# Seven half products that go on accumulating in PSUM, with ScalarE as the copier and another order of products

## The chip, the core and the metric

The kernel runs on one core of a Trainium2 chip. The metric is the device time of one execution in microseconds (us). TensorE (PE in the profile, its weight loads PEld) multiplies and writes to the PSUM banks; VectorE (DVE), ScalarE (ACT) and GpSimd (POOL) work beside it, each through its own queue in order; SyncE (SP) issues most DMAs.

## What is computed

One step of a two-layer trunk over 1024 prompt tokens and 64 sample tokens: a Mamba-2 layer, then a layer of causal window sums, each with a gated mixer and a residual add, then a final norm. The part that matters here is the large projections:

```python
def ssd_branch(h, ...):
    zxbcdt = h @ w_in              # 1024 -> 6176: z (gate), x, B, C, dt
    ...
    xbc_act = jax.nn.silu(conv)    # a causal convolution of width 4 over x, B, C
    ...
def pool_branch(h, ...):
    uz = h @ w_in                  # 1024 -> 4096: u (2048 columns) and z (2048 columns)
    ...                            # window sums of u over 4, 8, 16 or 2 tokens; silu(z)
```

All of it is float32, and the outputs are float32 too.

## The kernel before

Activations lie with features on the 128 partitions and the 1088 tokens (TOK) along the free axis. A float32 product is made of three matmuls: weights and activations are each split into a rounded high part and the rest, and high x high, high x low and low x high are summed in PSUM.

**Pairs of output tiles by seven half products.** For 12 pairs of the front (the list FRONT: pairs "z" of the gate, pairs "b" and "x" that feed the convolution) and for 14 pairs of the pool layer (p = 2 to 15) two output tiles u and z of 128 x 1088 are made together in Winograd's form of Strassen's product: the inner size 1024 and the tokens are halved, and seven products of 128 x 512 by 512 x 544 take the place of eight. Their activation operands are called B11, B21, T2, T3, T1, T4 and B22; the T are sums of blocks that were made ahead. A half product is 24 matmuls of 128 x 272 (2 halves of the tokens, c = 0 and 1; 4 blocks of the inner size; 3 of the split): lines L980 to L982 in `product`. A pair is 168 matmuls.

**The weights.** `w_sums` is a generator: each `next` gives one half weight operand, in the order of the products. GpSimd forms the sums of weight blocks (L945, L946, L950, L952), and `split_half` makes the high part by a ScalarE copy (L174) and the low part by a subtraction on VectorE, or on GpSimd for two of every seven (L176). `product` asks for the operand three products ahead; there are four buffers for split operands (tags wh and wl, two each), so a split can be made when the product four before it is done.

**Evacuation.** `fast_pair` runs the products as B11, B21, T2, T3, T1, T4, B22, each into PSUM banks of its own (tags mm, tr, y, S: eight banks in all). ScalarE copies B11 to a tile `s` (L1006); after that VectorE adds each product's banks to `s`, to z or to u (the adds all stand at L991, in a helper), 14 adds of 128 x 272 a pair, one more where the sample tokens lie apart.

**Work behind a pair.** `after(x)` is called behind each product. In the front, behind B22 of a "b" or "x" pair, the convolution of both tiles is written (`proj_end`, `conv_tile`): per tile a ScalarE start (L351, a part of 1024 tokens and one of 64), three VectorE steps on each part (L349), and an activation on ScalarE (L352). Six of the 12 front pairs have it. Gate pairs take an activation (`z_chunk`, L862) and a store. In the pool layer `u_pool` follows a pair: a chain of window sums on VectorE (L845, L850, L852, L854) and a store. In the first two front pairs the steps of `dt_phase` are interleaved; the last ends in small transposes on TensorE.

**Order.** The program is traced into a scheduler, which fixes each engine's queue ahead of the run; the listing's order is its order of preference among what is ready. `issue_after` pins a few instructions. On the chip every queue then runs in order and waits on semaphores.

Of the kernel before, what the change touches and what calls it, by code (L numbers as in the profile page):

```python
# [7 lines left out]
F32 = mybir.dt.float32  # L8
F32R = mybir.dt.float32r
AF = mybir.ActivationFunctionType  # L10
# [4 lines left out]
P = 128  # L15
# [82 lines left out]
class Build:  # L98
# [837 lines left out]
    def w_sums(self, n):  # L936


        nc = self.nc
        for _ in range(n):  # L940
            u, z = self.stream_next_raw(), self.stream_next_raw()
            self.stream_raw(self.wpos)
            s = self.tp.tile([P, 8, P], F32, tag="sw", bufs=2, name=self.name("sw"))
            f, l = slice(0, 4), slice(4, 8)
# [8 lines left out]
            yield self.split_half(s[:, f])  # L953
            yield self.split_half(z[:, l])
            self.stream_raw(self.wpos + 1)
            yield self.split_half(s[:, l])

    def fast_init(self, n):
# [4 lines left out]
        self.X = {"B11": [(h[:, :HALF], l[:, :HALF]) for h, l in self.hn[:4]], "T1": [(h[:, HALF:], l[:, HALF:]) for h, l in self.hn[:4]],  # L963
                  "B21": [(h[:, :HALF], l[:, :HALF]) for h, l in self.hn[4:]], "B22": [(h[:, HALF:], l[:, HALF:]) for h, l in self.hn[4:]]}

    def product(self, tags, x):
        nc = self.nc
        if x not in self.X:
            self.X[x] = [(t[:, :HALF], t[:, HALF:]) for t in (self.T[int(x[1]), k] for k in range(4))]
        nxt = next(self.wgen, None)  # L970
        if nxt:
            self.wahead.append(nxt)
        else:
            self.stream_split(self.wpos)
        hi, lo = self.wahead.pop(0)
        ps = [self.pp.tile([P, 512], F32, tag=t, bufs={"mm": 3, "tr": 2, "y": 2, "S": 1}[t], name=self.name("st")) for t in tags]
        for c in range(2):
            t = slice(QUART * c, QUART * c + QUART)
            for k, (xh, xl) in enumerate(self.X[x]):
                nc.tensor.matmul(ps[c][:, :QUART], hi[:, k], xh[:, t], start=(k == 0), stop=False)  # L980
                nc.tensor.matmul(ps[c][:, :QUART], hi[:, k], xl[:, t], start=False, stop=False)  # L981
                nc.tensor.matmul(ps[c][:, :QUART], lo[:, k], xh[:, t], start=False, stop=(k == 3))  # L982
        return [q[:, :QUART] for q in ps]

    def fast_pair(self, u, z, after):


        nc, product = self.nc, self.product

        def add(out, x, y):  # L990
            nc.vector.tensor_tensor(out=out, in0=x, in1=y, op=ALU.add)  # L991

        def put(dst, half, c, x, y):
            t, o, rv = dst
            o += HALF * half + QUART * c
            n = QUART - NS if rv is not None and half and c else QUART
            add(t[:, o:o + n], x[:, :n], y[:, :n])
            if n < QUART:
                add(rv, *(v[:, n:].rearrange("p (b i) -> p b i", i=8) for v in (x, y)))

        cs = [slice(QUART * c, QUART * c + QUART) for c in range(2)]
        s = self.tp.tile([P, HALF], F32, tag="mt2", bufs=self.nmt2, name=self.name("u2"))
        z1 = z[0][:, z[1]:z[1] + HALF]
        ps = product(("mm", "mm"), "B11")
        for c in range(2):
            nc.scalar.activation(s[:, cs[c]], ps[c], AF.Copy)  # L1006
        after("B11")
        ps = product(("tr", "tr"), "B21")
        for c in range(2):
            put(u, 0, c, ps[c], s[:, cs[c]])  # L1010
        after("B21")
        ps = product(("y", "y"), "T2")
        for c in range(2):
            add(s[:, cs[c]], ps[c], s[:, cs[c]])
        after("T2")
        ps = product(("mm", "S"), "T3")
        for c in range(2):
            add(z1[:, cs[c]], ps[c], s[:, cs[c]])
        after("T3")
        ps = product(("mm", "mm"), "T1")  # L1020
        for c in range(2):
            add(s[:, cs[c]], ps[c], s[:, cs[c]])
            put(z, 1, c, ps[c], z1[:, cs[c]])
            after(f"z1{c}")
        after("T1")
        ps = product(("tr", "tr"), "T4")
        for c in range(2):
            put(z, 0, c, ps[c], z1[:, cs[c]])
            after(f"z0{c}")
        after("T4")  # L1030
        ps = product(("y", "y"), "B22")
        for c in range(2):
            put(u, 1, c, ps[c], s[:, cs[c]])
        after("B22")

    def fast_pairs(self, late):

        sl = self.slots
        self.fast_init(16 - PLAIN)
        for p in range(PLAIN, 16):  # L1040
            U, dst = self.u_begin(p), sl.get("pz")

            def after(x):
                if x in ("z01", "z11"):
                    a = HALF * int(x[1])
                    self.z_chunk(dst, dst[:, a:a + HALF], a, HALF)
                elif x == "T4":
                    self.z_store(p, dst)
                elif p == 15 and x in ("T2", "T3"):
                    sl.free(*[self.T[int(x[1]), k] for k in range(4)])  # L1050
                    if x == "T2":
                        self.group_load(0)
                elif p == 15 and x == "T1":
                    self.free_acts(self.hn[:4])

            self.fast_pair((U[0], 15, U[1][:, :, 15:23]), (dst, 0, None), after)
            if p - PLAIN < len(late):
                self.u_pool(p - PLAIN, late[p - PLAIN])
            if p < 15:
                self.u_pool(p, U)  # L1060
        self.free_acts(self.hn[4:])
        sl.free(*[self.T[4, k] for k in range(4)])
        return U

    def group_load(self, gi):

# [342 lines left out]
    def front_pairs(self, ops, dt):  # L1409

        nc, sl = self.nc, self.slots
        self.fast_init(len(FRONT))
        self.G, G = {}, None
        for n, (kind, g) in enumerate(FRONT):
            if kind == "z":
                ts = [sl.get("z") for _ in range(2)]
                outs = [(t, 0, None) for t in ts]
            else:
                if kind == "b":
                    self.G[g] = G = self.proj_open(g)  # L1420
                ii = 2 * (kind == "x")
                ts = [self.proj_begin(G, ii + i) for i in range(2)]
                outs = [(t, 3, t[:, 1027:1115].rearrange("p (b w) -> p b w", w=11)[:, :, 3:11]) for t in ts]

            def after(x):
                if kind == "z" and x in ("z01", "z11"):
                    a = HALF * int(x[1])
                    self.z_chunk(ts[1], ts[1][:, a:a + HALF], a, HALF)
                elif kind == "z" and x in ("B21", "B22"):
                    a = HALF * (x == "B22")  # L1430
                    self.z_chunk(ts[0], ts[0][:, a:a + HALF], a, HALF)
                    if x == "B22":
                        self.gate_store(2 * g, ts[0])
# [9 lines left out]
                if n == 0 and x in ("B11", "B21"):  # L1443
# [11 lines left out]
            self.fast_pair(*outs, after)  # L1455
        sl.free(*[self.T[4, k] for k in range(4)])

    def ssd_layer(self):
# [348 lines left out]
```

## Time and profile before

| | |
|---|---|
| median of 3 runs | 1625.97 us (1620.98 to 1626.91) |
| the profiled execution | 1625.1 us, span 1623.2 us |
| granted TensorE clock, mean | 0.995 |
| PE busy | 1594.8 us, 98% of the span, 12061 matmuls |
| PEld busy | 1519.9 us, 94% |
| DVE busy | 1290.4 us, 79% |
| ACT busy | 815.2 us, 50% |
| POOL busy | 497.8 us, 31% |

The front's 12 pairs stand between 95.75 and 354.5 us of the span, the pool layer's 14 pairs between 1051.58 and 1346.5 us. A row of the timeline gives start, duration, engine, line, operation, output and inputs by the program's names, shape and count; in square brackets stands the engine's idle time before it and who ended it. Consecutive rows of one line are merged, with the last end. A row of groups gives the busy sum and the mean of one instruction, then the idle time before them. Matmuls are pipelined, so the duration of one (288 ns) is longer than the distance to the next.

### The profile page before, as it was taken

The numbers are of one execution on the slowest core, as the hardware profiler recorded it, in microseconds if no ns is written. First come the engines' busy times: TensorE is split into PE (matmuls) and PEld (weight loads), VectorE is DVE, ScalarE is ACT, GpSimd is POOL, SyncE is SP. The second block draws the span as 40 slices with busy tenths as digits, with TensorE's granted clock in tenths as the row PEclk, the third lists the DMA queues.
The fourth block names the chain that finished last, engine by engine and source line by source line (L and its number), as shares of the span: only waits on it lengthen the run. The fifth ranks groups of instructions, "written<-read, shape, count | busy, mean of one in ns | idle before, by whom it ended". The sixth has DMA issues, their size and how long they took to land.

```text
span 1623.2 us, 30975 instructions
## 1 busy us (share of the span) xinstructions
PE 1594.8 (98%) x12061; PEld 1519.9 (94%) x12061; DVE 1290.4 (79%) x2140; ACT 815.2 (50%) x1565; POOL 497.8 (31%) x527
## 2 busy tenths in 40 slices
PE   8999999999999999999999999999999999999997
PEld 6899999998889898898899899999999999999997
DVE  6875779777787888889878867988899867577886
ACT  6653444357667667675555536632322233333364
POOL 0233556421221302120112222366667640000241
PEclk9999999999999999999999999999999999999999
DMA  9422232354554554678899633043333369665773
GB/s 348 163 99 82 94 110 71 107 198 128 194 161 159 166 190 134 215 226 295 272 333 313 216 130 112 29 143 111 103 108 100 134 206 362 181 159 182 160 175 121
DMA packets 122306, 275.60 MB, mean 170 GB/s; under 512 B 18192, under 2 KB 59312, under 8 KB 122160
## 3 DMA queue, kind: packets, MB, share of 16 engines
q1 hardware_dynamic: 118128, 260.91, 47.4%
q0 software_dynamic: 4032, 12.72, 4.5%
q8 instruction: 95, 1.56, 0.4%
q14 instruction: 51, 0.42, 0.1%
HBM read 201.12 MB, written 70.23 MB: 167 GB/s over the span
## 4 chain that ended last, share of the span: by engine, by line
PE 83%; DVE 6%; DMA 4%; issue 3%; ACT 3%; POOL 1%; SPq 0%; DVEq 0%; POOLq 0%; ACTq 0%
PE st L982 11%; PE st L980 11%; PE st L981 11%; PE mm L182 10%; PE mm L183 10%; PE mm L184 10%; PE op L1197 2%; PE op L1198 2%; PE op L1196 2%; PE y L609 2%; PE S L588 2%; PE y L613 1%; DMA acb<-acd 1%; PE am L253 1%; PE tr L549 1%
## 5 line engine op out<-in xcount | busy, mean ns | idle before, releaser
L982 PE MATMUL st<-hh,w 128*128 128x272 f32 x832 | 240.8, 289 | 2.3 <-DVE w L176 2.3
L980 PE MATMUL st<-hh,w 128*128 128x272 f32 x832 | 240.2, 289 | 0.0
L981 PE MATMUL st<-hl,w 128*128 128x272 f32 x832 | 239.8, 288 | 0.0
L982 PE MATMUL st<-t,w 128*128 128x272 f32 x624 | 179.5, 288 | 0.0
L980 PE MATMUL st<-t,w 128*128 128x272 f32 x624 | 179.5, 288 | 0.0
L981 PE MATMUL st<-t,w 128*128 128x272 f32 x624 | 179.2, 287 | 0.0
L182 PE MATMUL mm<-hh,wh 128*128 128x368 f32 (+1 forms) x528 | 178.2, 338 | 0.1
L183 PE MATMUL mm<-hl,wh 128*128 128x368 f32 (+1 forms) x528 | 173.4, 328 | 0.0
L184 PE MATMUL mm<-hh,wl 128*128 128x368 f32 (+1 forms) x528 | 173.4, 328 | 0.0
L174 ACT ACTIVATE w<-wr 128x512 fp32r<-128x512 f32 x104 | 65.7, 631 | 190.1 <-PE st L982 156.7
L982 PEld LDWEIGHTS st<-hh,w 128*128 128x128 f32 x832 | 156.4, 188 | 3.4 <-DVE w L176 3.4
L980 PEld LDWEIGHTS st<-hh,w 128*128 128x128 f32 x832 | 156.7, 188 | 0.3 <-issue 0.3
L981 PEld LDWEIGHTS st<-hl,w 128*128 128x128 f32 x832 | 156.8, 188 | 0.0
L596 POOL TENSOR_TENSOR hd<-h,cd 128x256 f32<-128x256 f32 x56 | 48.7, 870 | 347.8 <-DVE h L597 190.5
L182 PE MATMUL mm<-gh,wh 128*128 128x368 f32 (+1 forms) x384 | 129.1, 337 | 0.6 <-ACT raw L419 0.6
L1197 PE MATMUL op<-b,w 128*128 128x272 f32 x448 | 128.9, 288 | 0.7 <-DVE b L1126 0.7
L1196 PE MATMUL op<-b,w 128*128 128x272 f32 x448 | 129.4, 289 | 0.0
L1198 PE MATMUL op<-b,w 128*128 128x272 f32 x448 | 128.9, 288 | 0.0
L183 PE MATMUL mm<-gl,wh 128*128 128x368 f32 (+1 forms) x384 | 126.0, 328 | 1.1 <-DVE gl L743 1.0
L184 PE MATMUL mm<-gh,wl 128*128 128x368 f32 (+1 forms) x384 | 126.0, 328 | 0.0
L980 PEld LDWEIGHTS st<-t,w 128*128 128x128 f32 x624 | 117.7, 189 | 0.0
L982 PEld LDWEIGHTS st<-t,w 128*128 128x128 f32 x624 | 117.3, 188 | 0.0
(293 smaller groups left out, 4610.4 us busy)
## 6 DMA issues: line engine op xcount, KB each, us to landing
wr<-win SPq DMA_DIRECT2D x48, 512.0 KB, 3.9
acb<-acd SPq DMA_DIRECT2D x64, 256.0 KB, 4.0
wr<-pin SPq DMA_DIRECT2D x32, 512.0 KB, 3.8
wr<-pout SPq DMA_DIRECT2D x28, 512.0 KB, 3.9
x<-x1d SPq DMA_DIRECT2D x24, 544.0 KB, 6.6
x1d<-x SPq DMA_DIRECT2D x22, 544.0 KB, 5.5
wr<-pout POOLq DMA_DIRECT2D x20, 512.0 KB, 5.5
x<-xT SPq DMA_DIRECT2D x16, 544.0 KB, 6.1
```

Of the source, the lines that this page charges most:

```text
L174: self.nc.scalar.activation(hi, src, AF.Copy)
L182: nc.tensor.matmul(ps[:, :n], hi[:, k, :], ah[:, a:a + n], start=first, stop=False)
L183: nc.tensor.matmul(ps[:, :n], hi[:, k, :], al[:, a:a + n], start=False, stop=False)
L184: nc.tensor.matmul(ps[:, :n], lo[:, k, :], ah[:, a:a + n], start=False, stop=last)
L588: nc.tensor.matmul(S[:, 256 * i:256 * i + 256], Bt, xde.rearrange("p r q -> p (r q)"), start=True, stop=True)
L596: nc.gpsimd.tensor_tensor(out=hd, in0=h[-1], in1=cd.unsqueeze(2).to_broadcast([P, 4, 64]), op=ALU.mult)
L980: nc.tensor.matmul(ps[c][:, :QUART], hi[:, k], xh[:, t], start=(k == 0), stop=False)
L981: nc.tensor.matmul(ps[c][:, :QUART], hi[:, k], xl[:, t], start=False, stop=False)
L982: nc.tensor.matmul(ps[c][:, :QUART], lo[:, k], xh[:, t], start=False, stop=(k == 3))
L1196: nc.tensor.matmul(ps[:, :QUART], hi[:, k], xh, start=k == 0, stop=False)
L1197: nc.tensor.matmul(ps[:, :QUART], hi[:, k], xl, start=False, stop=False)
L1198: nc.tensor.matmul(ps[:, :QUART], lo[:, k], xh, start=False, stop=k == 7)
```

## The change

`fast_pair` becomes `fast_run`, which runs all pairs of a stage.

- Partial sums stay in PSUM: T2, T1 and B22 are added by TensorE onto the banks of B11 (A), and T4 onto those of T3 (E); the first matmul of such a product does not start a new sum.
- ScalarE copies the state of the banks out between products: A after B11 (to `s`), A after T2 (to the first half of z), E after T3 (to `v`). VectorE adds only three times, for B21, T1 and T4. At the end ScalarE copies A to u, with the activation for gate pairs in the same instruction.
- The order in a pair is B11, T2, T3, B21, T1, T4, B22, and B11 of the next pair comes between T1 and T4; `w_sums` gives the operands in that order, and the next pair's first weight block is loaded earlier.
- What follows a pair (`after("B22")`, in the pool layer `u_pool`) stays behind B22.

```diff
     def w_sums(self, n):
...
-            yield self.split_half(u[:, f])
-            yield self.split_half(u[:, l])
             yield self.split_half(s[:, l])
             nc.gpsimd.tensor_tensor(out=z[:, f], in0=u[:, f], in1=z[:, f], op=ALU.subtract)
             yield self.split_half(z[:, f])
             nc.gpsimd.tensor_tensor(out=s[:, l], in0=u[:, l], in1=s[:, l], op=ALU.subtract)
+            yield self.split_half(u[:, l])
             yield self.split_half(s[:, f])
+            if i + 1 < n:
+                u = self.stream_next_raw()
+                self.stream_raw(self.wpos)
+                yield self.split_half(u[:, f])
             yield self.split_half(z[:, l])
-            self.stream_raw(self.wpos + 1)
             yield self.split_half(s[:, l])
...
-    def product(self, tags, x):
+    def product(self, ps, x, more=False):
...
-                nc.tensor.matmul(ps[c][:, :QUART], hi[:, k], xh[:, t], start=(k == 0), stop=False)
...
+                nc.tensor.matmul(ps[c], hi[:, k], xh[:, t], start=(k == 0 and not more), stop=False, skip_group_check=True)
...
+    def fast_run(self, n, make):
...
+        def first(i):
+            A = banks(*(("y", "y"), ("mm", "mm"))[i % 2])
+            product(A, "B11")
+            s = self.tp.tile([P, HALF], F32, tag="mt2", bufs=self.nmt2, name=self.name("m1"))
+            for c in range(2):
+                copy(s[:, cs[c]], A[c])
+            return A, s
+
+        A, s = first(0)
+        for i in range(n):
+            u, z, after = make(i)
+            after("B11")
+            z1 = z[0][:, z[1]:z[1] + HALF]
+            product(A, "T2", True)
+            for c in range(2):
+                copy(z1[:, cs[c]], A[c])
+            after("T2")
+            E = banks("mm", "S")
+            product(E, "T3")
+            v = self.tp.tile([P, HALF], F32, tag="mt2", bufs=self.nmt2, name=self.name("m7"))
+            for c in range(2):
+                copy(v[:, cs[c]], E[c])
+            after("T3")
+            B = banks("tr", "tr")
+            product(B, "B21")
+            for c in range(2):
+                put(u, 0, c, B[c], s[:, cs[c]])
+            after("B21")
+            product(A, "T1", True)
+            for c in range(2):
+                put(z, 1, c, A[c], v[:, cs[c]])
+                after(f"z1{c}")
+            after("T1")
+            nxt = first(i + 1) if i + 1 < n else None
+            product(E, "T4", True)
+            for c in range(2):
+                put(z, 0, c, E[c], z1[:, cs[c]])
+                after(f"z0{c}")
+            after("T4")
+            product(A, "B22", True)
+            for c in range(2):
+                for o, w in parts(u, 1, c):
+                    nc.scalar.activation(o, w(A[c]), u[3])
+            after("B22")
+            if nxt:
+                A, s = nxt
```

`copy` is a ScalarE activation (Copy), `put` a VectorE add. The steps of `dt_phase` and of the activation sums (`ops`) hang on the same names of products as before, save that the second step of `ops` comes behind T2 in place of B21.

More of the change, by code (lines that the diff above doesn't have):

```diff
@@ L975, in product @@
         hi, lo = self.wahead.pop(0)
-        ps = [self.pp.tile([P, 512], F32, tag=t, bufs={"mm": 3, "tr": 2, "y": 2, "S": 1}[t], name=self.name("st")) for t in tags]
         for c in range(2):
@@ L979, in product @@
             for k, (xh, xl) in enumerate(self.X[x]):
[L980 to L991, printed above, removed]
-        def put(dst, half, c, x, y):
[L994 to L1034, printed above, removed]
@@ new lines, in product, with parts, copy @@
+                nc.tensor.matmul(ps[c], hi[:, k], xh[:, t], start=(k == 0 and not more), stop=False, skip_group_check=True)
+                nc.tensor.matmul(ps[c], hi[:, k], xl[:, t], start=False, stop=False, skip_group_check=True)
+                nc.tensor.matmul(ps[c], lo[:, k], xh[:, t], start=False, stop=(k == 3), skip_group_check=True)
+    def fast_run(self, n, make):
+        nc, product, banks = self.nc, self.product, self.banks
+        cs = [slice(QUART * c, QUART * c + QUART) for c in range(2)]
+        def parts(dst, half, c):
+            t, o, rv = dst[:3]
+            o += HALF * half + QUART * c
+            m = QUART - NS if rv is not None and half and c else QUART
+            out = [(t[:, o:o + m], lambda v: v[:, :m])]
+            if m < QUART:
+                out.append((rv, lambda v: v[:, m:].rearrange("p (b i) -> p b i", i=8)))
+            return out
+        def put(dst, half, c, x, y):
+            for o, v in parts(dst, half, c):
+                nc.vector.tensor_tensor(out=o, in0=v(x), in1=v(y), op=ALU.add)
+        def copy(out, x):
+            nc.scalar.activation(out, x, AF.Copy)
+        def first(i):
[6 more added lines that the diff above has]
+        A, s = first(0)
+        for i in range(n):
+            u, z, after = make(i)
[34 more added lines that the diff above has]
+                A, s = nxt
@@ L1039, in fast_pairs, with make @@
         self.fast_init(16 - PLAIN)
-        for p in range(PLAIN, 16):
+        last = []
+        def make(i):
+            p = PLAIN + i
             U, dst = self.u_begin(p), sl.get("pz")
@@ L1428, in after @@
                     self.z_chunk(ts[1], ts[1][:, a:a + HALF], a, HALF)
[L1429 to L1433, printed above, removed]
+                elif kind == "z" and x == "B21":
+                    self.z_chunk(ts[0], ts[0][:, :HALF], 0, HALF)
+                elif kind == "z" and x == "B22":
+                    self.gate_store(2 * g, ts[0])
                 elif kind == "z" and x == "T4":
@@ L1442, in after @@
                             sl.free(t)
-                if n == 0 and x in ("B11", "B21"):
+                if n == 0 and x in ("B11", "T2"):
                     next(ops)
```

41 lines of the change are left out of this document (25 added, 16 removed).

## The prediction

> **What bounds the kernel now.** I read the page first, then a table of the two stages that the change touches, then PE's waits, then the engines around one wait.
>
> ```profile
> span 1623.2 us, 30975 instructions
> ...
> PE 1594.8 (98%) x12061; PEld 1519.9 (94%) x12061; DVE 1290.4 (79%) x2140; ACT 815.2 (50%) x1565; POOL 497.8 (31%) x527
> ```
>
> TensorE has work for 98% of the span, so a change that keeps all its matmuls can win only what TensorE still waits. The windows show how much that is (columns: stretch, length, busy us and count of PE, PEld, DVE, ACT, POOL, granted clock, DMA share, GB/s).
>
> ```profile
> 95.75:354.50 258.75, 256.49 (x2039) 254.45 (x2038) 196.32 (x329) 110.64 (x176) 124.77 (x119) 1.00 0.31 104
> 182.37:204.11 21.74, 21.32 (x170) 21.10 (x169) 21.44 (x34) 10.24 (x15) 13.07 (x14) 1.00 0.32 101
> 225.84:246.89 21.05, 21.05 (x171) 21.05 (x170) 11.75 (x24) 7.24 (x12) 8.86 (x8) 1.00 0.25 89
> 1051.58:1346.50 294.92, 294.92 (x2354) 294.92 (x2353) 248.77 (x368) 96.04 (x165) 175.83 (x136) 1.00 0.40 134
> ```
>
> The last row is the pool layer's fast stage: 14 pairs of 7 x 24 = 168 matmuls, TensorE without a gap, 294.92 / 14 = 21.07 us a pair, 3.01 us a half product. Nothing can be won there. The first row is the front's: 12 pairs would take 252.8 us at that pace and take 258.75, so 5.9 us is all that this change could win in the front. The third row is a front pair without a wait (21.05), the second one with a wait (21.74). In it VectorE is busy 21.44 of 21.74 us. The list of PE's waits (total, times, longest) names the instruction:
>
> ```profile
> PE st L982 <- DVE w L176: 2.3, 5, 0.6
> ```
>
> Five times a product waits for the low part of its weights, which VectorE makes by a subtraction (L176). The timeline shows which product and why. First TensorE, from the pair's first matmul:
>
> ```profile
> 182.37 0.28 PE L980 MATMUL st<-hh,w 128*128 128x272 f32 x1
> ...
> 194.42 0.29 PE L980 MATMUL st<-hh,w 128*128 128x272 f32 x1
> 194.55 0.29 PE L981 MATMUL st<-hl,w 128*128 128x272 f32 x1
> 195.25 0.39 PE L982 MATMUL st<-hh,w 128*128 128x272 f32 x1 [0.42 <-DVE w L176]
> ```
>
> 194.42 is 12.05 us after 182.37: four half products, so this is T1, the fifth. Its third matmul, the first with the low part, was due at 194.68 and began at 195.25: 0.57 us late. VectorE meanwhile:
>
> ```profile
> 181.44 2.00 DVE L349 SCALAR_TENSOR_TENSOR xbc<-raw,vec,xbc 128x1024 f32<-128x1024 f32 x1
> 183.37 0.49 DVE L991 TENSOR_TENSOR raw<-st,u 128x208 f32<-128x208 f32 x2
> 183.78 10.80 DVE L349 SCALAR_TENSOR_TENSOR xbc<-raw,vec,xbc 128x1024 f32<-128x1024 f32 x8
> 194.51 0.68 DVE L176 TENSOR_TENSOR w<-sw,w 128x512 fp32r<-128x512 f32 x1
> ```
>
> The convolution of the pair just finished (L349) holds VectorE until 194.51, then comes T1's subtraction, and 0.74 us after its start the matmul goes. ScalarE had made the high part long before:
>
> ```profile
> 183.76 1.57 ACT L351 ACTIVATE xbc<-raw,vec 128x1024 f32<-128x1024 f32 x2 [0.52 <-DVE raw L991]
> 185.25 0.74 ACT L1006 ACTIVATE u<-st 128x272 f32<-128x272 f32 x2
> 185.88 0.62 ACT L174 ACTIVATE w<-sw 128x512 fp32r<-128x512 f32 x1
> ...
> 193.43 2.31 ACT L352 ACTIVATE xbc<-xbc 128x1088 f32<-128x1088 f32 x2 [4.11 <-DVE xbc L349]
> ```
>
> The high part (L174) was ready at 186.50, and the subtraction still stood behind eight convolution steps for 8.0 us. In the code the convolution is written behind the last product of its pair and T1's split behind the second product of the next pair: the earlier written work went first. In the last front pair the same eight steps are shorter, and TensorE did not wait:
>
> ```profile
> 333.32 0.29 PE L980 MATMUL st<-hh,w 128*128 128x272 f32 x1
> ...
> 334.72 8.72 DVE L349 SCALAR_TENSOR_TENSOR xbc<-raw,vec,xbc 128x1024 f32<-128x1024 f32 x8
> 343.37 0.68 DVE L176 TENSOR_TENSOR w<-sw,w 128x512 fp32r<-128x512 f32 x1
> ```
>
> **The change, part by part.** Matmuls: as many, of the same shapes, so nothing. The flags for accumulation and the skipped group check add no instruction: nothing.
>
> Work moved from VectorE to ScalarE. A pair's two-operand adds fall from 14 to 6, ScalarE's copies rise from 2 to 8:
>
> ```profile
> L991 DVE TENSOR_TENSOR u<-st,u 128x272 f32<-128x272 f32 x146 | 60.5, 432 | 24.0 <-PE st L982 21.7
> L1006 ACT ACTIVATE u<-st 128x272 f32<-128x272 f32 x52 | 20.2, 394 | 32.1 <-PE st L982 32.1
> ```
>
> VectorE loses 8 x 0.432 = 3.5 us a pair, ScalarE gains 6 x 0.394 = 2.4 us. ScalarE is busy 110.64 / 12 = 9.2 us a front pair and 6.9 us a pool pair of 21, so it has the room. Neither is on the path by its sum: worth nothing directly. What counts is what stands in the queue before a split.
>
> The order. Between two pairs TensorE now runs B11 of the next pair, T4, B22, and then T2, T3, B21, T1. The convolution still follows B22, and its start hangs on T4 and B22 as before (third and second last product, before and after). But only three products now lie between B22 and T1, where there were four. T1's low part is needed 3.01 us sooner: its third matmul is due 9.03 + 0.26 = 9.29 us after B22's end, not 12.31. Of the convolution block only the two adds of B22 leave (from 183.37 to 183.78, 0.41 us). Its end moves from 194.51 - 182.37 = 12.14 to 11.73 us, the matmul can go 0.74 us later, at 12.47: a wait of 3.18 us in place of 0.57. For five pairs that is 5 x 2.61 = 13.05 us. In the last pair: 343.37 - 333.32 = 10.05, less 0.41, plus 0.74, gives 10.38 against 9.29: 1.09 us, where there was none. Together +14.1 us. What is late behind T1 is only T1: T4's and B22's splits stand next in VectorE's queue and have two and three products more.
>
> The clock. A wait of 3 us may also cost clock. Four windows at the start of the pool layer and around one longer idle time:
>
> ```profile
> 906.90:910.30 3.40, 2.10 (x25) 1.83 (x27) 1.29 (x4) 0.59 (x3) 0.61 (x1) 1.00 0.96 330
> 1016.10:1019.50 3.40, 1.46 (x8) 0.88 (x7) 1.74 (x5) 2.11 (x7) 2.87 (x10) 1.00 0.00 0
> 1019.50:1022.90 3.40, 3.39 (x12) 3.40 (x13) 3.40 (x14) 3.40 (x13) 1.05 (x3) 0.50 0.00 0
> 1022.90:1026.30 3.40, 3.40 (x22) 3.40 (x22) 3.40 (x11) 2.64 (x8) 0.49 (x1) 0.99 0.00 0
> ```
>
> A window with PE busy for 1.46 of 3.40 us was followed by one at half the clock, with 12 matmuls where the next had 22: 10/22 of 3.40, 1.5 us lost. A window with 2.10 busy was not. A wait of 3.18 us leaves at most about 1.8 us of work in one of the two windows on which it falls, so each of the five may or may not trip it: between 0 and 7.5 us, I take three of five, 4.6 us. [...]
>
> New waits on ScalarE's copies. T1 adds to the banks that T2's copies read, T4 to those that T3's copies read, B22 to those that T1's adds read; between each lie two products, 6.0 us, against a copy of 0.39. The one long hold on ScalarE is the activation behind the convolution (L352, 4.11 us above); T3's copies may wait there, and T4 comes 9 us after them. Nothing. Only at a stage's first pair does T2 follow B11 directly:
>
> ```profile
> 1054.59 0.29 PE L980 MATMUL st<-hh,w 128*128 128x272 f32 x1
> ...
> 1054.99 0.67 ACT L1006 ACTIVATE u<-st 128x272 f32<-128x272 f32 x2
> ```
>
> B11 ended at 1054.59, and its first copy would end at 1054.99 + 0.39, 0.8 us after. Bounds 0 and 1.6 for two stages; I take 0.8, because in the pool layer the row stands.
>
> The pool layer. Its VectorE chain behind B22 (window sums, L845) has one operand after another, and the trace shows that a split gets in between:
>
> ```profile
> 1199.81 1.43 DVE L845 TENSOR_TENSOR ws<-u 128x1222 f32<-128x1222 f32 x1
> 1201.27 3.87 DVE L845 TENSOR_TENSOR ws<-ws 128x1220 f32<-128x1220 f32 x2
> 1205.06 1.78 DVE L176 TENSOR_TENSOR w<-sw,w 128x512 fp32r<-128x512 f32 x1
> ```
>
> So T1's split should pass at the next step, well before 9.29 us: nothing. If it had to wait for the whole chain in the four widest pairs, about 1 us each, 4 us.
>
> The loads. The next pair's first weight block is fetched half a pair sooner; the DMA engines are 0.31 busy there: nothing. The pair with the transposes of dt keeps its place, behind the fourth product: nothing, bounds -2.4 and +1 (the 5.9 us less five waits of 0.7).
>
> Sum: 14.1 + 4.6 + 0.8 = 19.5 us on the profiled 1625.1 (span 1623.2 and 1.9 around it), 1644.6; the median of the runs shown is 0.9 higher. I say 1645. Its own range is 1637 (no clock loss, blocks a little shorter) to 1650.
>
> **The rivals.** First, the split passes: T1's high part is free to be made as soon as B22's weights are done, so its subtraction could get in before the block closes. Then the five waits vanish: -2.9 + 0.8, about 1624, not slower. For it: the pool rows just shown, and 3.5 us less on VectorE. Against it: 194.51, where a ready split waited 8.0 us because two tiles' chains alternate; and ScalarE makes the high part only after both L351 steps, 1.57 us, by which time the second chain runs. It decides if the high part is ready before that second chain, about 2 us after B22.
>
> Second, the block is as short as in the last pair everywhere (GpSimd's work falls otherwise): 6 x 1.09 - 2.9 + 0.8 = +4.4, 1630, and no clock loss.
>
> Third, inside the forecast, no window of the clock trips: 14.9 us in all, 1640; I give it a quarter of the forecast's chance, 0.13.
>
> Fourth, the pool layer waits too: 4 us more and perhaps a window of clock, 1650 to 1655.
>
> **How the numbers follow.** Forecast 0.52 (0.13 of it without a clock loss), the split passes 0.23, short block 0.15, pool layer too 0.07, anything else 0.03. The range 1623 to 1651 holds the first three and leaves out the rest. About 0.5% (8.1 us) is what a measurement of this kernel can tell from no change. Faster by that would need more than the 5.9 us that are there: 0.02. Within it lie the passing split and nearly all of the short block: 0.39. Slower: 0.59.
>
> **What would show it.** Right: PE's wait for DVE w L176 grows from 2.3 to some 16 us, at the product T1, in six pairs; the pairs behind a convolution take about 24 us; some windows after them show 0.50 clock; the pool stage stays at 294.9 us; each pair has eight VectorE adds fewer and six ScalarE copies more. Wrong: those waits gone (first rival), about 1 us each (second), or a wait for ACT copies, which I put at nothing.

## The result, and the profile after

The changed kernel takes 1650.15 us (median of four runs, 1648.84 to 1653.8) where the kernel before takes 1626.44 us beside it (1620.98 to 1627.01). The ratio is 1.0157, interval 1.0129 to 1.0185: slower, by 24 us between the medians and by 21 to 30 us by the interval. On the time of the prediction that is 1651.5 us, 6.5 us above the forecast of 1645 and just outside its range. A second comparison, with further runs of both kernels, gave 1.0132, 1.0104 to 1.0161.

The page's head, then the five stretches of the profiled run: up to the first fast matmul, the front's 12 pairs, the stretch between, the pool layer's 14 pairs, the rest (columns as before):

```profile
span 1647.1 us, 30656 instructions
...
PE 1602.4 (97%) x12061; PEld 1525.9 (93%) x12061; DVE 1208.0 (73%) x1912; ACT 860.7 (52%) x1735; POOL 482.0 (29%) x527
```

```profile
0.00:96.62 96.62, 88.72 (x629) 74.80 (x630) 72.70 (x136) 59.67 (x91) 11.71 (x11) 0.96 0.60 222
96.62:368.95 272.33, 260.54 (x2036) 258.30 (x2036) 161.91 (x230) 129.14 (x249) 116.64 (x118) 0.98 0.28 97
368.95:1068.96 700.01, 689.37 (x5113) 631.73 (x5112) 568.96 (x960) 436.27 (x980) 144.85 (x208) 1.00 0.58 195
1068.96:1369.37 300.41, 296.46 (x2354) 295.14 (x2353) 201.79 (x246) 123.60 (x262) 163.93 (x135) 1.00 0.39 129
1369.37:1647.10 277.73, 267.32 (x1939) 265.93 (x1937) 202.69 (x343) 111.98 (x157) 44.86 (x55) 0.99 0.65 188
```

VectorE has lost 82 us of work and TensorE has as many matmuls, yet the span is 23.9 us longer. Cut at the same instructions, the kernel before took 95.75, 258.49, 697.34, 294.87 and 276.75 us. So the front is 13.8 us longer, the pool stage 5.5, and the three stretches in which the change touches nothing 4.5 together. The front's granted clock is 0.98, where it was 1.00.

TensorE's waits in the two stages (total, times, longest):

```profile
PE st L990 <- DVE w L176: 11.8, 5, 2.6
PE st L988 <- ACT pz L862: 2.4, 1, 2.4
PE st L990 <- POOL w L176: 1.2, 4, 0.3
PE st L990 <- POOL u L822: 0.3, 1, 0.3
```

The first row answers to the row of 2.3 us before (the matmul with the low part, L982, is L990 now). The others are new. The last is one more wait at the same matmul (the third of the next pair's B11), which the profile puts down to another GpSimd instruction. A row counts idle time from the modelled end of the matmul before; by the starts of the products the delay of the second row is 2.7 us, and that of the last two is 0.55 to 0.6 us in each of five pool pairs. The timeline shows the first kind behind B22, which ended at 186.50; TensorE, ScalarE and VectorE in turn:

```profile
195.64 0.29 PE L989 MATMUL st<-hl,w 128*128 128x272 f32 x1
198.47 0.59 PE L990 MATMUL st<-hh,w 128*128 128x272 f32 x1 [2.54 <-DVE w L176]
...
188.56 0.62 ACT L174 ACTIVATE w<-sw 128x512 fp32r<-128x512 f32 x1
...
185.56 12.25 DVE L349 SCALAR_TENSOR_TENSOR xbc<-raw,vec,xbc 128x1024 f32<-128x1024 f32 x9 [1.42 <-ACT xbc L351]
197.73 0.68 DVE L176 TENSOR_TENSOR w<-sw,w 128x512 fp32r<-128x512 f32 x1
```

T1's high part was ready at 189.18. Its subtraction stood behind the convolution until 197.73, 8.5 us, and the matmul went 0.74 us after its start: 2.7 us late. T1 is late by 2.7 us in four pairs, by 1.7 in a fifth, and not at all in the sixth.

What such a wait did to the clock differed with how it lay to windows of 3.41 us, as the rows show. In the trace of the changed kernel five stretches between 60 and 1600 us are at half clock, each 3.41 us long, from 197.99, 269.67, 293.56, 925.03 and 1037.67 us on; these starts lie 21, 7, 185 and 33 times 3.413 us apart. The windows here are cut on such a grid, that of each trace's half clock. The changed kernel around this wait, then a later wait of the same length in a second run of the same kernel:

```profile
194.58:197.99 3.41, 1.35 (x11) 1.13 (x9) 3.41 (x5) 0.14 (x1) 2.07 (x4) 1.00 0.00 0
197.99:201.40 3.41, 2.93 (x13) 2.94 (x14) 2.59 (x6) 1.49 (x2) 0.49 (x1) 0.50 0.57 175
201.40:204.81 3.41, 3.41 (x29) 3.41 (x29) 1.93 (x6) 1.36 (x3) 0.84 (x3) 1.00 0.36 142
```

```profile
218.17:221.58 3.41, 1.54 (x13) 1.32 (x11) 3.41 (x5) 0.00 (x0) 2.16 (x2) 1.00 0.00 0
221.59:225.00 3.41, 2.74 (x22) 2.74 (x23) 2.87 (x7) 2.30 (x3) 0.61 (x2) 1.00 0.48 157
```

In the first, a window with 1.35 us of work was followed by one at half clock; in the second, one with 1.54 was not. Three of the five waits of the profiled run were followed by such a window, none in the second run.

### The profile page after: what moved, and what is told of

Read it like the earlier page. It is cut to its first block, busy times and chain, and to the rows that moved or that the text cites. A ratio compares the mean times of both kernels' runs of the same rounds, so it can differ in the third digit from the quotient of the medians.

```text
span 1647.1 us, 30656 instructions
## 1 busy us (share of the span) xinstructions
PE 1602.4 (97%) x12061; PEld 1525.9 (93%) x12061; DVE 1208.0 (73%) x1912; ACT 860.7 (52%) x1735; POOL 482.0 (29%) x527
## 4 chain that ended last, share of the span: by engine, by line
PE 74%; DVE 9%; DMA 5%; issue 4%; POOL 4%; ACT 3%; SPq 0%; DVEq 0%; POOLq 0%; ACTq 0%
PE mm L182 10%; PE mm L183 9%; PE mm L184 9%; PE st L990 9%; PE st L988 9%; PE st L989 9%; DVE xbc L349 3%; PE op L1229 2%; PE op L1230 2%; PE op L1228 2%; DMA acb<-acd 2%; PE y L609 2%; PE S L588 2%; PE y L613 1%; PE am L253 1%
## 5 line engine op out<-in xcount | busy, mean ns | idle before, releaser
L990 PE MATMUL st<-hh,w 128*128 128x272 f32 x832 | 243.3, 292 | 13.3 <-DVE w L176 11.8
L990 PE MATMUL st<-t,w 128*128 128x272 f32 x624 | 179.6, 288 | 0.0
L990 PEld LDWEIGHTS st<-hh,w 128*128 128x128 f32 x832 | 158.5, 190 | 15.5 <-DVE w L176 12.9
L988 PEld LDWEIGHTS st<-hh,w 128*128 128x128 f32 x832 | 158.6, 191 | 3.0 <-ACT pz L862 2.7
L988 PEld LDWEIGHTS st<-t,w 128*128 128x128 f32 x624 | 117.6, 188 | 0.1
L990 PEld LDWEIGHTS st<-t,w 128*128 128x128 f32 x624 | 117.4, 188 | 0.0
L989 PEld LDWEIGHTS st<-t,w 128*128 128x128 f32 x624 | 117.2, 188 | 0.0
```

What stands on the lines that cost most here:

```text
L988: nc.tensor.matmul(ps[c], hi[:, k], xh[:, t], start=(k == 0 and not more), stop=False, skip_group_check=True)
L989: nc.tensor.matmul(ps[c], hi[:, k], xl[:, t], start=False, stop=False, skip_group_check=True)
L990: nc.tensor.matmul(ps[c], lo[:, k], xh[:, t], start=False, stop=(k == 3), skip_group_check=True)
```

## The experiments

Two theories. A: what counts is where a weight's low part stands in the queue that makes it, against how soon its product comes. B: what costs is the new evacuation, summing in PSUM with ScalarE as the copier. All runs in one table; front and pool stage are cut as above, from one trace each. A ratio is against the kernel before on the same chip, so ratios compare better across rows than medians do.

| kernel | median us | ratio to before | interval | front us | pool stage us |
|---|---|---|---|---|---|
| before | 1626.44 | | | 258.5 | 294.9 |
| before, second trace | 1627.8 | 1.0005 | 0.9984 to 1.0027 | 258.6 | 294.9 |
| changed | 1650.15 | 1.0157 | 1.0129 to 1.0185 | 272.3 | 300.4 |
| changed, second run | 1648.53 | 1.0132 | 1.0104 to 1.0161 | 268.4 | 300.4 |
| convolution late | 1632.88 | 1.0032 | 1.0020 to 1.0044 | 255.5 | 301.7 |
| no product ahead | 1634.19 | 1.0040 | 1.0025 to 1.0055 | 255.9 | 301.2 |
| new order, old evacuation | 1654.9 | 1.0169 | 1.0152 to 1.0185 | 286.3 | 296.3 |
| high parts first | 1635.44 | 1.0049 | 1.0029 to 1.0068 | 259.5 | 299.1 |
| other banks at the entry | 1651.22 | 1.0148 | 1.0125 to 1.0171 | 272.4 | 302.0 |
| GpSimd's split moved | 1636.92 | 1.0064 | 1.0043 to 1.0084 | 264.2 | 299.2 |
| before, convolution late | 1627.94 | 0.9995 | 0.9977 to 1.0013 | 257.2 | 294.9 |
| three edits | 1630.52 | 1.0024 | 1.0013 to 1.0035 | 256.2 | 298.4 |
| four edits | 1627.67 | 1.0006 | 0.9992 to 1.0020 | 255.2 | 296.1 |
| before, high parts first | 1626.55 | 0.9997 | 0.9987 to 1.0008 | 254.8 | 295.2 |

**The changed kernel again.**

> The changed kernel once more, for a second trace beside the same runs of the kernel before. Theory A (T1's low weight part waits behind the convolution in VectorE's queue, and some of these waits trip the clock gate): the front stage is again about 13 to 15 us longer than before, with PE's waits for DVE w L176 at some 12 us. Theory B (the lengthening of 2.7 us between the two stages, where nothing was changed, belongs to the change): that part is again 2.7 us longer. If it is a chance of the transfers and of the clock windows, it lies anywhere within about 3 us of before.

The waits were the same 11.8 us in five. The front took 268.4 us instead of 272.3, since no window at half clock followed: the three windows cost 4.0 us. The stretch between the two stages took 700.5 us, about 3 us longer than before, as in the first run; what that means is taken up under "Before again".

**The convolution late.** The changed kernel, with the convolution written behind T2 of the next pair, where T1's split already stands in VectorE's queue:

```diff
+                if x == "T2" and self.late:
+                    self.late.pop()()
...
-                    for i in range(2):
-                        self.proj_end(G, ii + i, ts[i])
...
+                    def conv():
+                        for i in range(2):
+                            self.proj_end(G, ii + i, ts[i])
...
+                    self.late.append(conv)
```

> The changed kernel with the convolution of a pair written behind T2 of the next pair, that is behind the split of T1's weights, and nothing else moved. Theory A: T1's low part now stands ahead of most of the convolution; the five waits of together 11.8 us and the three clock windows of 1.5 us in the front go, and the time falls by 12 to 16 us, to about 1636. Theory B (the partial sums in PSUM and ScalarE's copies hold TensorE): the front stays some 13 us longer than before, since none of that is changed.

Its VectorE behind a B22 that ended at 187.26, the front, and TensorE's waits:

```profile
188.84 0.68 DVE L176 TENSOR_TENSOR w<-sw,w 128x512 fp32r<-128x512 f32 x1
189.44 9.63 DVE L349 SCALAR_TENSOR_TENSOR xbc<-raw,vec,xbc 128x1024 f32<-128x1024 f32 x7
```

```profile
97.38:352.85 255.47, 255.30 (x2036) 253.92 (x2035) 159.92 (x230) 127.79 (x249) 122.80 (x118) 1.00 0.32 104
```

```profile
PE st L988 <- ACT pz L862: 2.5, 1, 2.5
...
PE st L990 <- POOL w L176: 1.4, 5, 0.4
```

The split went first, no wait for VectorE is left, and the front is 3 us shorter than before the change, with all of the new evacuation in it. That is theory A. The kernel is still 0.3% slower: the pool stage keeps its loss.

**No product ahead.** The changed kernel with the next pair's B11 behind B22 again; sums in PSUM and copies stay. The weights come in that order too, so each engine's splits fall on other products:

```diff
-        A, s = first(0)
         for i in range(n):
             u, z, after = make(i)
+            A, s = first(i)
...
-            nxt = first(i + 1) if i + 1 < n else None
...
-            if nxt:
-                A, s = nxt
```

> The changed kernel with B11 of the next pair back behind B22, so four products lie again between a pair's end and T1; the accumulation in PSUM, ScalarE's copies and the order T2, T3, B21, T1 stay. Theory A: T1's low part is due 3.0 us later, 12.3 us after B22, against a convolution that lets it go at about 12.0; the waits of T1 go to nearly nothing and the front is within 3 us of before, the whole about 1636. Against that stand new waits: T2 follows B11 at once and needs ScalarE's copies, which may stand behind the activation of the convolution; these could cost up to 1 us a pair. Theory B: still some 13 us in the front.

```profile
PE st L983 <- ACT pz L862: 2.5, 1, 2.5
PE st L985 <- POOL w L176: 1.3, 1, 1.3
```

With four products between B22 and T1 again, T1's waits are gone and the front takes 255.9 us. So it was the product moved ahead that made T1 late. GpSimd's part, which moved too, can account for 1 us of the 2.7 at most ("GpSimd's split moved" below). The feared waits for ScalarE's copies, with T2 directly behind B11 in every pair, came to about 0.1 us a pair.

**The new order with the old evacuation.** Every product into banks of its own again, VectorE adds, but B11 of the next pair ahead of T4 and B22:

```diff
-            product(A, "T2", True)
+            ps = half(("y", "y"), "T2")
...
-                copy(z1[:, cs[c]], A[c])
+                add(v[:, cs[c]], ps[c], s[:, cs[c]])
...
-            product(A, "T1", True)
+            ps = half(("y", "y"), "T1")
```

> The kernel before's way of taking the products out (every product in banks of its own, VectorE's adds, one ScalarE copy), in the changed order with B11 of the next pair ahead of T4 and B22. Theory A: the order alone makes the loss: T1 waits in five or six pairs by 3 us, a little more than in the changed kernel, because B22's adds stand in the convolution again and VectorE has 3.5 us more a pair; the front is 15 to 20 us longer than before, the whole 1643 to 1652. Theory B: about as before, 1626.

```profile
PE st L988 <- DVE m L1012: 18.4, 6, 3.6
```

```profile
95.91:382.19 286.28, 267.87 (x2036) 265.63 (x2035) 198.30 (x331) 111.21 (x177) 125.80 (x118) 0.95 0.28 93
```

The front is 27.8 us longer than before, where 15 to 20 was expected, and 18 us longer than in the second run of the changed kernel. T1 now waits at its first matmul, for banks that T2's adds (L1012) have still to read, and these adds stand behind the convolution. With this choice of banks the new evacuation helps in this order: ScalarE reads those banks while VectorE is busy. For the front, theory B falls.

**High parts first.** In each half product the 16 matmuls with the weights' high part ahead of the 8 with the low part:

```diff
             for k, (xh, xl) in enumerate(self.X[x]):
                 nc.tensor.matmul(ps[c], hi[:, k], xh[:, t], ...)
                 nc.tensor.matmul(ps[c], hi[:, k], xl[:, t], ...)
+        for c in range(2):
+            t = slice(QUART * c, QUART * c + QUART)
+            for k, (xh, xl) in enumerate(self.X[x]):
                 nc.tensor.matmul(ps[c], lo[:, k], xh[:, t], ...)
```

> The changed kernel with only the order of the matmuls inside each half product altered: the 16 with the high part of the weights (both banks) come ahead of the 8 with the low part, so the low part is needed about 16 x 0.125 - 0.26 = 1.7 us later. As many matmuls of the same shapes; queues and splits as they are. Theory A (the low part of T1's weights, made behind the convolution in VectorE's queue, sets the wait): the five waits of 2.7 us fall to about 0.9 us each, no window at half clock follows in the front, the 0.5 us waits of the pool layer go, since they are shorter than the shift: front 258 to 260 us, pool stage 297 to 298, the median 12 to 17 us under the changed kernel, about 1634. Theory B (ScalarE's copies and the summing in PSUM are what costs): no fewer waits, the same 1650; the high part of T1 would be what is missing, and the waits would stand at L988.

```profile
PE st L993 <- DVE w L176: 3.2, 4, 0.8
PE st L988 <- ACT pz L862: 3.0, 1, 3.0
```

The four long waits fell to 0.8 us and less, the fifth went, the waits for GpSimd went, and no half clock followed in the front. The wait at the pool stage's entry stayed: it is for a bank. Only the point at which the low part is needed was moved, and that took some 14 us off.

**Other banks at the entry.**

```diff
-            A = banks(*(("y", "y"), ("mm", "mm"))[i % 2])
+            A = banks(*(("y", "y"), ("mm", "mm"))[(i + (self.nmt2 == 3)) % 2])
```

> The changed kernel, with the first pair of the pool layer starting in the banks tagged mm in place of y; nothing else differs. The 2.4 us wait for ScalarE's activation L862 at the pool stage's start should go, since the tile made just before it holds only the y banks: pool stage 300.4 to 297.7 us. The front stays 268 to 272 us, the waits of T1 stay. In time -2.7 us, which is at the edge of what is measured: the trace decides. If the wait goes on at the same place with another releaser, the bank was not the cause but ScalarE's lateness was (the copies of B11 stand behind the same splits).

The pool stage's start in the changed kernel, TensorE and then ScalarE:

```profile
1070.34 0.29 PE L990 MATMUL st<-hh,w 128*128 128x272 f32 x1
1073.06 0.40 PE L988 MATMUL st<-hh,w 128*128 128x272 f32 x1 [2.43 <-ACT pz L862]
...
1069.31 0.65 ACT L907 ACTIVATE t<-x 128x544 fp32r<-128x544 f32 x1
1069.86 2.28 ACT L907 ACTIVATE hh<-x 128x544 fp32r<-128x544 f32 x4
1072.04 0.62 ACT L174 ACTIVATE w<-wr 128x512 fp32r<-128x512 f32 x1
1072.56 0.45 ACT L862 ACTIVATE pz<-pl 128x352 f32<-128x352 f32 x1
```

The second half of B11 waits for a bank of the plain tile made just before it; ScalarE empties that bank (L862) only behind five activation splits (L907) and a weight split (L174). With the other banks:

```profile
PE st L990 <- POOL w L176: 1.9, 4, 1.0
PE st L988 <- ACT m L1012: 1.7, 1, 1.7
```

The wait for L862 is gone, and T2 waits 1.7 us for the copies of B11 (L1012), which stand behind the same splits. The bank chose the victim; ScalarE's lateness was the cause, as the last sentence of the expectation allowed. The 1.7 us are a cost of the new evacuation itself: in the kernel before, no product adds to banks from which ScalarE has still to copy. Only 0.7 us was to be had. A window at half clock, and one wait for GpSimd of 1.0 us in place of 0.3, took back more than that: the stage got longer, 302.0 us. In the runs "convolution late", "no product ahead", "high parts first", "GpSimd's split moved" and "three edits" the wait at the entry was followed by half clock too, so their pool stages hold such a window, which the changed kernel's two traces don't.

**GpSimd's split moved.** Two of each seven low parts are made on GpSimd, by their number in the order of products. The change reordered the products, and so the two fell on B21 and on the next pair's B11, where they had been T3 and T4. Here the second is T4's again:

```diff
-POOLW = (3, 5)
+POOLW = (3, 6)
```

> The changed kernel, with GpSimd making the low parts of the products 4 and 7 of each seven (T4 in place of the next pair's B11; T1's number and the others keep their engine). By the trace of the changed kernel five pool pairs wait 0.45 to 0.55 us each for the low part of the next pair's B11, made on GpSimd behind its sums. Expected: those waits of 2.6 us go, if VectorE has the part ready, pool stage 300.4 to about 298 us; if GpSimd is simply behind its due times, the wait moves to the product it now makes. In the front one more split falls on VectorE or moves by one place: T1's waits 2.7 us as before, or longer by the 0.68 us of a subtraction.

The pool waits for GpSimd went, as expected. That T1's waits in the front fell to 1.6 us was not expected. One step of the convolution in the changed kernel, with what GpSimd did then, and the same step here:

```profile
195.32 2.29 DVE L349 SCALAR_TENSOR_TENSOR xbc<-raw,vec,xbc 128x1024 f32<-128x1024 f32 x1
...
195.23 1.30 POOL L176 TENSOR_TENSOR w<-wr,w 128x512 fp32r<-128x512 f32 x1
```

```profile
195.76 1.27 DVE L349 SCALAR_TENSOR_TENSOR xbc<-raw,vec,xbc 128x1024 f32<-128x1024 f32 x1
```

```profile
PE st L990 <- DVE w L176: 7.8, 5, 1.6
```

Beside GpSimd's subtraction the same step took 1.0 us more. Without it the convolution ended that much sooner in four of the five pairs, and a wait of 1.6 us was nowhere in the front followed by half clock. One digit took 12 to 13 us off the median (1636.92 against 1648.53 and 1650.15). In the rows above, the step that began 0.09 us after GpSimd's subtraction ended 1.1 us after it, nearly its own 1.27 us; by what mechanism the one holds up the other is not shown.

**Before, with the convolution late.** The same edit as above in the kernel before, behind its B21:

```diff
+                if x == "B21" and self.late:
+                    self.late.pop()()
```

> The kernel before, with one edit: the convolution of a finished pair is written behind the fourth product of the next pair (B21 in its order is second: behind that product's call), that is behind the split of T1's weights, instead of directly behind B22. Theory A: the five waits of 0.57 us go, the front falls from 258.5 to about 255.6 us, like the front of the changed kernel with the convolution late (255.5), and the kernel is 3 us faster than before, 1624 to 1625. If the front of this one stays at 258.5, the 3 us gained in that other kernel came from the change itself and not from the place of the convolution.

```profile
PE st L980 <- ACT w L174: 0.9, 2, 0.5
PE st L982 <- DVE w L176: 0.4, 2, 0.2
```

T1's five waits went. In two pairs B22 came late instead, first for its high part, made on ScalarE, and then for its low part, and the front fell by 1.3 us, not 3. No difference in time was measured: the expected gain of 3 us is a miss.

**Three edits, and four.** The changed kernel with the convolution late, the other banks at the entry and GpSimd's split moved; then also with the high parts first.

> The changed kernel with three edits together: the convolution behind T2 of the next pair, the first pair of the pool layer in the mm banks, GpSimd making T4's low part in place of the next pair's B11. Theory A, summed over the stages: front 255.5 us (three us under the kernel before), pool stage 299 us (a wait of 1.7 to 2.5 us at its start stays, the 2.6 us of waits for GpSimd go), the rest as in the other kernels: 1629 to 1631 us beside 1627 of the kernel before, ratio 1.001 to 1.002. If it lies over 1635, the places of the loss have been read wrongly.

> The three edits and, in each half product, the 16 matmuls with the weights' high part ahead of the 8 with the low part. No product of the front or the pool stage should wait for a low part; front 255 us, pool stage 297.5 us, 1627 to 1629 us in all, ratio to the kernel before 1.000 to 1.001. The seven products with summing in PSUM are then as fast as the old evacuation, and no faster, since TensorE is full in both.

The four edits, front and pool stage, and the one wait for another engine's work that is left in them:

```profile
96.31:351.49 255.18, 255.18 (x2036) 253.99 (x2035) 163.06 (x230) 129.91 (x249) 121.89 (x118) 1.00 0.32 104
1050.21:1346.32 296.11, 294.30 (x2354) 294.08 (x2353) 204.55 (x246) 124.46 (x263) 153.62 (x135) 1.00 0.40 130
```

```profile
PE st L988 <- ACT m L1015: 1.8, 1, 1.8
```

The front runs without a gap, and the kernel is level with before: 1.0006, 0.9992 to 1.0020. Both medians came out as expected. The four edits give back all that can be measured of the loss. Nothing is won beyond it: the 5.9 us of the front are TensorE's only idle time that they could reach, and the entry takes 1.8 of that back.

**Before, with the high parts first.** The same three lines as above in the kernel before.

> The kernel before with one edit: in each half product the 16 matmuls with the weights' high part ahead of the 8 with the low part. Its five waits of 0.57 us for T1's low part are shorter than the 1.7 us by which the low part is needed later: they go, the front falls from 258.5 to about 255.5 us, pool stage 294.9 us as before, 1624 to 1625 us, ratio 0.998. If it beats both kernels, it does so by at most the 5.9 us that the front has over the pool's pace.

```profile
96.00:350.77 254.77, 254.77 (x2037) 253.82 (x2035) 190.74 (x329) 110.24 (x176) 126.37 (x119) 1.00 0.31 103
```

The front lost all its waits and 3.7 us, more than expected, but the median did not move: 0.9997, 0.9987 to 1.0008. The three untouched stretches took 1074.8 us in this trace beside 1069.8 before. Whether the edit lengthens them or they merely vary stays open. No version here beats the kernel before.

**Before again.**

> The kernel before, unchanged, for a second trace of it. Between the front's last product and the pool stage's first the change touches nothing, yet this stretch took 697.3 us in the first trace of before and 698.7 to 702.6 us in most others. If that is spread from run to run, this trace shows another value, 697 to 702 us; if it shows 697.3 again, the 2.7 us there may belong to the change. The front should again take 258.5 us with five waits of 0.57 us, the pool stage 294.9 us.

The stretch between took 694.7 us, where the first trace had 697.3 and the kernel before with a late convolution 702.6, all with the same code in it. That is another value, as the first reading had it, and even below its 697 to 702 us. The front (258.6) and the pool stage (294.9) stayed. So what this stretch takes differs by some 8 us between traces with the same code in it, and its 2.7 us can't be put down to the change.

## Why the prediction was right in kind and failed in two steps

The profiled runs of before and after, term by term in us:

| step of the prediction | predicted | measured |
|---|---|---|
| T1 behind the convolution | +14.1 | +9.5 (11.8 less 2.3) |
| clock | +4.6 (three windows) | +4.0 (three windows; front of the first less the second run) |
| entry of the pool stage | +0.8 | +2.7 |
| low parts in the pool stage | 0 | +2.8 |
| stretches the change doesn't touch | 0 | +4.5 |
| left over in the front | 0 | +0.3 |
| sum, before rounding | 19.5 | 23.9 |

**T1's wait: right in mechanism, too long.** The instruction, the product and the 0.74 us from the split to the matmul came as said. The size failed at "only the two adds of B22 leave (0.41 us)": the convolution ended 197.73 - 186.50 = 11.23 us after B22, not 11.73. Its remaining eight steps could start 0.38 us after B22, where the prediction's rows had them at 1.41. Besides the adds, the first of the nine steps had become shorter: it began 0.9 us before B22's end in both kernels, but took 2.00 us before (the row of 181.44), beside a GpSimd sum of weights that began at 181.06, and 1.28 us now. The fifth and the sixth block, to be compared with the 12.25 us above:

```profile
327.29 11.24 DVE L349 SCALAR_TENSOR_TENSOR xbc<-raw,vec,xbc 128x1024 f32<-128x1024 f32 x9 [1.42 <-ACT xbc L351]
350.12 9.13 DVE L349 SCALAR_TENSOR_TENSOR xbc<-raw,vec,xbc 128x1024 f32<-128x1024 f32 x9 [1.42 <-ACT xbc L351]
```

In the fifth, GpSimd came to its split only at the block's end. The sixth had no wait where 1.09 was said: no pair follows in the front, so GpSimd has no weights to sum, and all six steps of 128x1024 took about 1.28 us, where three of six took 2.3 in the first block. The length of the convolution, which the prediction took from the rows of before as fixed, differed with what GpSimd did beside it: 12.25, 11.24 and 9.13 us in these rows, and by 1.0 us in one step in the run "GpSimd's split moved"; its second rival had named this.

**The clock: right, and by chance in its count.** Three of five windows was the guess, three the count, none in the second run. The rows above show a drop after a window with 1.35 us of work, which is what the prediction's row with 1.46 had pointed to. The same wait of 2.54 us left 1.35 us of work in its window in one run and 1.54 us in the other, and only in the first did half clock follow.

**The entry: a failed step.** The prediction looked for the new wait at T2 behind B11's copies and took 0.8 us from a trace in which ScalarE was less far behind. It did not ask which tags B11's banks have at the first pair: with y they are those of the plain tile before it. The kind it named came out in the run with other banks, at 1.7 us: ScalarE's queue is late there in either case. Part of that lateness is new. ScalarE began to empty the bank (L862) 3.60 us after the stage's first matmul, and 2.55 us after it in the kernel before. Two rows of the changed kernel, then two of the kernel before:

```profile
1066.44 1.27 DVE L850 TENSOR_TENSOR ws<-ws,kc 128x3 f32<-128x3 f32 x1
1063.37 4.33 POOL L953 TENSOR_TENSOR sw<-wr,sw 128x512 f32<-128x512 f32 x1 [9.57 <-DVE w L176]
...
1049.07 0.15 DVE L850 TENSOR_TENSOR ws<-ws,kc 128x3 f32<-128x3 f32 x1
1054.13 0.45 ACT L862 ACTIVATE pz<-pl 128x352 f32<-128x352 f32 x1
```

In the new order a GpSimd sum of weights runs ahead of the stage. Beside it a VectorE step of 128x3 took 1.27 us; it took 0.15 before, with GpSimd idle, and ScalarE's splits (L907) hang on what VectorE makes behind that step. No run moves this sum alone, so that it accounts for the 1.05 us is read from the rows and not shown.

**The pool stage's "nothing": the other failed step.** It weighed only T1's split in VectorE's queue, which indeed never waited. It did not follow GpSimd's share, which goes by number and so moved to the next pair's B11 without a line of the diff naming it. In five pairs that low part came 0.55 to 0.6 us late, and its place cost another 1 us in each of four pairs of the front, inside T1's wait. The fourth rival (the pool layer waits too) had a cost of the right size by another mechanism.

**The untouched stretches.** They took 1074.4 us after and 1075.6 in its second run; with the same code before, 1069.8, 1069.1, 1077.2 and 1074.8. The 4.5 us lie within what traces with the same code there differ by and are not put down to the change.

**How near the sum came is luck.** T1 and the clock were 5.2 us too high, the entry and the pool stage's low parts 4.7 us too low, so the two stages lost about 19.4 us where 19.5 was forecast. The traced time lies above that by the stretches that the change doesn't touch. By the second comparison the time would be 1647.4 us, inside the range; by the first it is just outside.

**The rest.** Matmuls (12061 as before), loads, copies' waits inside a pair and the transposes of dt cost nothing, as said: no row of TensorE's waits in the two stages names them. The first rival (the split passes) was made true by the late convolution: the front came out 3 us shorter, as it said, but not its 1624 us, because of the pool stage.

## What to carry to other kernels

A reordering moves everything that counts its turn: which engine makes operand number five, which bank the first of a stage gets, how many products lie between a long block and the operand behind it. Go through these for the new order one by one, the ends of a stage too. Before shortening a queue's block, see whether the needed operand can be written ahead of the block or be used later in its product.

## What the runs showed of the hardware

On the clock the traces hold more than the prediction's rows. In the new order with the old evacuation:

```profile
272.39:275.80 3.41, 1.54 (x12) 1.58 (x13) 3.41 (x8) 2.34 (x3) 1.44 (x3) 1.00 0.56 225
275.80:279.21 3.41, 3.41 (x17) 3.41 (x16) 2.33 (x7) 0.24 (x1) 0.00 (x0) 0.50 0.77 256
```

Here 1.54 us of TensorE work in a window was followed by half clock; in the second run of the changed kernel the same 1.54 was not. Over the windows of 3.41 us between 60 and 1600 us of all fourteen traces, cut on the grid of each trace's half clock, each one at full clock with 1.53 us of work or less (29 of them) was followed by half clock and none with 1.75 or more; of the fourteen from 1.54 to 1.70 six were followed by it and eight were not. The prediction had only the ends 1.46 and 2.10. From these counts it is an estimate that a wait of up to 3.41 - 1.75 = 1.66 us, alone in its window, costs only itself; one of 2.7 us cost 1.3 us more (4.0 for three) or nothing, by how it lay to the windows. And beside GpSimd's subtraction a VectorE step took 2.29 us, without it 1.27 us, which set the end of a whole block; beside a GpSimd sum a step of 128x3 took 1.27 us, and 0.15 us in the kernel before with GpSimd idle.
